# An adaptive-sum task, transfers through DRAM and the last mixed rows of a two-layer hybrid backbone on one Trainium2 core

## The chip, the cores and the metric

The kernel runs on one core of one Trainium2 chip. A core has a matrix engine (TensorE, PE in the profile; its weight loads are shown apart as PEld), VectorE (DVE), ScalarE (ACT), GpSimd (POOL) and SyncE (SP), which issues most of the transfers between DRAM and on-chip memory. Each engine carries out its own list of instructions in the order in which the program wrote them, and waits where an instruction needs something that another engine or a transfer has not finished. The measure is the device time of one execution in microseconds (us), lower being better; the time before is the median of three.

## The reference, cut to what matters

Two layers run over 256 latent tokens x and 256 context tokens ctx, each 2,048 wide, all in 32-bit floating point. Each layer starts with a normalization whose shift, scale and final gate are computed from one conditioning vector c ("adaptive" values): a product of a vector with a 2,048 x 6,144 matrix for each layer.

```python
def adaln(cond, w, b):
    m = jax.nn.silu(cond) @ w + b
    return jnp.split(m, 3, axis=-1)            # shift, scale, gate

for i in range(DEPTH):                          # DEPTH = 2
    shift, scale, gate = adaln(c, ada_w[i], ada_b[i])
    h = modulate(rms_norm(x, norm_g[i]), shift[:, None], scale[:, None])
    ...
    y = na_ssd_mixer(...) if i % 2 == 0 else short_conv_mixer(...)
    x = x + gate[:, None] * y
```

Layer 0 projects h into queries, keys, values, gates and the inputs of a state-space scan (SSD) with one large matrix; 16 heads do two-dimensional neighbourhood attention over latent and context tokens, and 32 heads of 64 do the scan in both directions. The results, 4,096 wide, are gated and the scan's half is normalized in 8 groups of 256 columns:

```python
def gated_group_rmsnorm(y, z, g):
    yz = (y * jax.nn.silu(z)).reshape(b, seq, SSD_GROUPS, -1)
    yz = yz * lax.rsqrt(jnp.mean(yz * yz, axis=-1, keepdims=True) + EPS)
    return yz.reshape(b, seq, SSD_WIDTH) * g
...
out = jnp.concatenate([ya, yb], axis=-1) @ w_out      # 4096 -> 2048
```

Layer 1 is a gated short convolution: four projections of h, a product of two of them convolved over three tokens, two gates, and an output projection.

## The kernel before

**Weights.** Each 32-bit product is made of three products of numbers split into a high and a low part. A weight tile of 512 KB is loaded by SP into one of five tiles called raw; ScalarE casts it into the high part wH (L423), VectorE subtracts that from the original into the low part wL (L430, in `low_part`), and TensorE multiplies (all products stand at L198, in the helper `mm`; transposes at L202, in `turn`). There are three buffers of wH and of wL. When `low_part` has been emitted, the raw tile is given back and `issue` emits the next load on SP. 452 such loads follow each other: layer 0's projections, then from load 228 on the output projection in three passes, and layer 1 from load 292 on, whose output projection is the last 32.

**What sets the order.** The program is written by generators ("tasks") that yield a condition before each piece: an engine, the tiles that the piece reads, and a number of PSUM banks, as in `yield W_("ACT", mx)`; "AQ" means ScalarE's DMA queue. They stand in three queues, urgent, side and back. The class `Plan` keeps a modelled clock for each engine and, for keys of 128 elements of a tile, when they were last written and read; `Plan.add` (L94 and following) advances it for each instruction emitted: a fixed cost by shape, or for a transfer a latency and the bytes at a rate. `may` decides from this model whether a task's next piece may be emitted already: the tiles must be ready, by the model, no later than about the engine's own time, which itself may run only some way ahead of TensorE (4500 ns for urgent, 2500 for side, 1500 for back). Where nothing may be emitted and the program cannot go on, `force` takes the piece that comes first. The model only fixes the order; on the chip each engine waits for what it needs. `cap` and `grow` set how many of ten tiles tmp (128x512) and nine tiles half (128x256) a task may hold.

**Adaptive sums.** The task `gemv_gen` in the queue back makes 16 vectors of 512 adaptive values, n = 0 to 15 (layer 0's gate, then layer 1's shift, scale and gate). For each it zeroes the tile acc on VectorE (L810), lets SP load a row of 512 bias values into acc's first partition (L811), and then consumes eight loads of ada_w, 512 KB each, which share the five raw tiles with the weights: two multiply-adds on VectorE per load (L820), 16 per vector. Four matmuls with ones add up the partitions, VectorE copies the result to rowb (L829) and ScalarE's queue sends it to the DRAM buffer mrow. Layer 1's start needs n = 11, its end n = 15.

**Scan groups.** For each of the 8 groups of scan heads, SP reads rows of cumulative sums from the DRAM buffer csr into tiles tmp, spread over 128 partitions (L1373, 256 KB each). ScalarE (L1383, L1390, L1393) and VectorE (L1387, L1398, L1401) make decay factors from them, and TensorE multiplies these with the inputs xtm. The group norm then takes the root on POOL (L1437), scales a 128x128 identity by it on VectorE (L1441, into a tile half), and multiplies ones with that on TensorE, so that the factor of each token stands in all partitions.

**Mixed rows.** Heads and scan groups give 32 blocks of 128 rows by 256 tokens ("mixed rows", 0 to 15 from attention and 16 to 31 from the scan), the input of the output projection. `put_mix` sends each to the DRAM buffer mixd on ScalarE's queue. Later three tasks `mixes` read them back in pairs, one tmp tile reserved to each task, and split each into high (ScalarE, L1538) and low (VectorE, L1539) in the memory where parts of h (tiles hH and hL) stood; a pair must therefore wait until these are free, which `free_rows` counts.

## Time and profile before

| what | us |
|---|---|
| median of three runs (lowest to highest) | 1801.51 (1799.98 to 1804.06) |
| time of the profiled execution | 1802.22 |
| span of the profiled execution | 1800.3 |
| TensorE busy | 1760.2 |
| VectorE busy | 1283.5 |
| ScalarE busy | 785.7 |
| POOL busy | 31.1 |
| mean granted TensorE clock | 0.998 of full |
| read from and written to DRAM | 372.89 MB and 11.96 MB |

All profile figures are of one execution. The span runs from its first to its last recorded instruction. A group of instructions is written as line, engine, operation, output<-input with buffer numbers left out, shape and type, then the number of them, their busy time in us and the mean in ns of one, and behind the second bar the idle time of the engine just before them with what ended it. A row of the timeline gives the start in us, the length, the engine, the line and the instruction; what stands in brackets is the engine's idle time before it and what ended it. In rows of waits the three numbers are the sum in us, how often, and the longest. A row of stretches gives the interval, then for PE, its weight loads, VectorE, ScalarE and POOL the busy time with the number of instructions, the idle time of all engines together, the granted TensorE clock, the DMA share and the GB/s. "SPq" is SP's DMA queue, "ACTq" ScalarE's.

### The profile page before, as it was taken

What the parts mean: (1) busy time and instruction counts of PE and PEld (TensorE: products, weight loads), DVE (VectorE), ACT (ScalarE), POOL (GpSimd) and SP (SyncE); (2) the same over time, 40 slices, a digit from 0 to 9 for tenths busy, and PEclk for the clock granted to TensorE, in tenths of its full rate; (3) what the DMA queues carried; (4) which work ended last, traced back from release to release, by engine and by line L of the source; (5) the groups of instructions that cost most, each with busy time, mean ns of one, the idle gap of its engine ahead of it and who ended that gap; (6) DMA issues with size and microseconds to landing.
All of it is one profiled execution on the core that took longest, in us unless ns stands there. A gap on an engine that the chain in (4) does not pass through costs nothing.

```text
span 1800.3 us, 25545 instructions
## 1 busy us (share of the span) xinstructions
PE 1760.2 (98%) x9545; PEld 1469.2 (82%) x9545; DVE 1283.5 (71%) x2049; ACT 785.7 (44%) x1354; POOL 31.1 (2%) x28
## 2 busy tenths in 40 slices
...
GB/s 347 340 291 254 194 168 126 156 206 194 211 161 190 162 174 204 191 158 167 172 219 120 163 188 194 232 209 295 273 184 232 260 278 268 270 237 265 220 220 167
DMA packets 260220, 385.23 MB, mean 214 GB/s; under 512 B 33424, under 2 KB 113008, under 8 KB 260096
## 3 DMA queue, kind: packets, MB, share of 16 engines
...
q14 instruction: 49, 0.40, 0.1%
HBM read 372.89 MB, written 11.96 MB: 214 GB/s over the span
## 4 chain that ended last, share of the span: by engine, by line
PE 89%; DMA 4%; DVE 4%; issue 1%; ACT 1%; SPq 0%; POOL 0%; ACTq 0%; POOLq 0%; DVEq 0%
PE bank L198 86%; PE bank L202 3%; DMA raw<-in_ada_w 2%; DVE wL L430 2%; DMA tmp<-dram_csr 1%; DVE acc L820 0%; DMA raw<-in_w_in 0%; DMA Dg<-dram_trd 0%; ACT wH L423 0%; DMA tmp<-in_x 0%; DMA xs<-in_x 0%; DVE hL L769 0%; DVE tmp L1398 0%; DVE tmp L1217 0%; DMA Du<-dram_trd 0%
## 5 line engine op out<-in xcount | busy, mean ns | idle before, releaser
L423 ACT CAST wH<-raw 128x1024 fp32r<-128x1024 f32 (+1 forms) x440 | 459.5, 1045 | 707.4 <-PE bank L198 606.5
L430 DVE TENSOR_TENSOR wL<-raw,wH 128x1024 fp32r<-128x1024 f32 (+1 forms) x440 | 530.5, 1212 | 225.9 <-ACT wH L423 224.1
L198 PE MATMUL bank<-hH,wH 128*128 128x256 f32 (+1 forms) x1040 | 342.7, 330 | 0.9 <-ACT wH L423 0.9
L198 PE MATMUL bank<-hL,wH 128*128 128x256 f32 (+1 forms) x1040 | 336.8, 324 | 0.0
L198 PE MATMUL bank<-hH,wL 128*128 128x256 f32 (+1 forms) x1024 | 331.3, 324 | 1.5 <-DVE wL L430 1.5
L198 PE MATMUL bank<-wH,h 128*128 128x512 f32 x1024 | 318.7, 392 | 2.1 <-DVE h L1662 1.7
L198 PE MATMUL bank<-wH,hH 128*128 128x512 f32 x640 | 257.2, 402 | 4.8 <-ACT hH L763 2.6
L820 DVE SCALAR_TENSOR_TENSOR acc<-raw,csil,acc 128x512 f32<-128x512 f32 x256 | 191.7, 749 | 91.0 <-DMA raw<-in_ada_w 74.0
L198 PE MATMUL bank<-wL,hH 128*128 128x512 f32 x640 | 249.8, 391 | 0.3 <-DVE wL L430 0.3
L198 PE MATMUL bank<-wH,hL 128*128 128x512 f32 x640 | 249.5, 390 | 0.1
L198 PEld LDWEIGHTS bank<-wH,h 128*128 128x128 f32 x1024 | 193.0, 189 | 44.3 <-DVE h L1662 3.0
L198 PEld LDWEIGHTS bank<-hH,wH 128*128 128x128 f32 x1040 | 197.6, 190 | 18.7 <-issue 2.0
L198 PEld LDWEIGHTS bank<-hL,wH 128*128 128x128 f32 x1040 | 197.7, 190 | 15.6
L198 PEld LDWEIGHTS bank<-hH,wL 128*128 128x128 f32 x1024 | 194.5, 190 | 17.8 <-DVE wL L430 2.5
L198 PE MATMUL bank<-wL,h 128*128 128x512 f32 x512 | 200.7, 392 | 5.4 <-DVE wL L430 5.4
L198 PE MATMUL bank<-wH,mix 128*128 128x512 f32 x512 | 162.7, 393 | 0.0
L198 PEld LDWEIGHTS bank<-wH,hH 128*128 128x128 f32 x640 | 120.2, 188 | 35.3 <-issue 6.5
L198 PEld LDWEIGHTS bank<-wH,hL 128*128 128x128 f32 x640 | 120.1, 188 | 25.6 <-DVE hL L769 0.6
L198 PEld LDWEIGHTS bank<-wL,hH 128*128 128x128 f32 x640 | 120.2, 188 | 24.8 <-DVE wL L430 1.1
L198 PEld LDWEIGHTS bank<-wL,h 128*128 128x128 f32 x512 | 96.6, 189 | 27.1 <-DVE wL L430 6.9
L198 PEld LDWEIGHTS bank<-wH,mix 128*128 128x128 f32 x512 | 96.1, 188 | 20.8 <-issue 0.9
L198 PE MATMUL bank<-wL,mix 128*128 128x512 f32 x256 | 99.8, 390 | 0.0
...
## 6 DMA issues: line engine op xcount, KB each, us to landing
...
raw<-in_sc_in SPq DMA_DIRECT2D x128, 512.0 KB, 4.4
...
tmp<-dram_csr SPq DMA_DIRECT2D x32, 256.0 KB, 6.2
...
```

The source lines that it names most:

```text
L198: E(T.matmul(o, l, r, start=start, stop=stop, skip_group_check=True))
L202: E(T.transpose(o, i, ident if k == 128 else ident[:k, :k]))
L423: E(S.copy(H, v))
L430: E(V.tensor_tensor(out=Lo, in0=v, in1=H.bitcast(F32), op=ALU.subtract))
L820: E(V.scalar_tensor_tensor(out=acc, in0=v[:, j], scalar=csil[:, 2 * k + j:2 * k + j + 1], in1=acc, op0=ALU.mult, op1=ALU.add))
```

## The change

**Plan.** In the model a transfer no longer waits for earlier writes of the tile that it writes, every transfer from or to a DRAM buffer counts as finished 3000 ns later, and the time at which a tile is written by a transfer only moves up. An engine's name with a "+" behind it ("DVE+", "ACT+") asks `may` to count the tiles as ready 1000 ns later than modelled.

**Sums.** The zeroing of acc is gone: the first of the 16 steps is a plain multiplication (tensor_scalar). The bias row goes into a tile of its own, adab, as four pieces of 128 on partitions 0, 32, 64 and 96, which POOL zeroes once at the start; it is added where the result is taken from PSUM, so the copy L829 becomes an addition of two operands. Pieces that consume a load ask for "DVE+".

**Mixed rows.** If the memory that a row goes to is already free when the row is finished, the new `place` splits it there at once, on ScalarE and VectorE, without the way through DRAM. In the order written, this is so for rows 12 to 15 and 28 to 31; the other 24 go through mixd as before and are read in 12 pairs. The tasks that read pairs take a tmp tile when they need it (`grow`, `cap`) instead of holding one each, and ask for "ACT+".

**Group norm.** The scaled identities (L1441) and the products of ones with them are replaced by transposes (`turn`) of the root's columns, each spread over 128 elements by reading with stride 0; TensorE's condition is now the root r2 itself.

Together VectorE has 16 memsets and 16 scalings fewer, and 16 of 256 multiply-adds are multiplications; ScalarE's queue has 12 reads of mixd instead of 16 and 24 writes instead of 32. TensorE's number of instructions is the same.

```diff
         for k in ko:
-            s = max(s, 0.0 if e == "PE" else self.w[k] + 60, self.r[k] + 60)
+            s = max(s, 0.0 if e == "PE" or op == "DMACopy" else self.w[k] + 60, self.r[k] + 60)
         if op == "DMACopy":
...
                 done = free = max(self.dma, s + 1000) + n / self.RATE + 1500
+            if any(a.tensor.name.startswith("dram") for a in ins + outs):
+                done = free = done + 3000
         else:
...
         for k in ko:
-            self.w[k] = done
+            self.w[k] = max(self.w[k], done) if op == "DMACopy" else done
             self.last[k[0]] = max(self.last[k[0]], done)
...
             return False
+        late = eng[-1] == "+"
+        eng = eng.rstrip("+")
         now, t = plan.t["PE"], plan.t["ACT" if eng == "AQ" else eng]
-        rdy = plan.ready(aps)
+        rdy = plan.ready(aps) + (1000 if late else 0)
         if eng == "AQ":
...
                             continue
-                        when_ = max(plan.t["ACT" if eng == "AQ" else eng], plan.ready(f))
+                        when_ = max(plan.t["ACT" if eng == "AQ" else eng.rstrip("+")], plan.ready(f))
                     if best is None or when_ < best[0]:
...
             c0 = 4096 + n * 512 if n < 4 else (n - 4) * 512
-            yield W_("DVE", nb=0)
-            E(V.memset(acc, 0.0))
-            E(DMA.dma_start(acc[:1, :], ada_b[lay:lay + 1, c0:c0 + 512]))
+            yield W_("SP")
+            E(DMA.dma_start(adab[0:128:32, :], ada_b[lay, c0:c0 + 512].rearrange("(g c) -> g c", g=4)))
             for k in range(8):
                 yield when(lambda: not (("gem", n, k) not in RAW))
-                yield W_("DVE", RAW["gem", n, k][1], acc)
+                yield W_("DVE+", RAW["gem", n, k][1])
                 raw, v = RAW.pop(("gem", n, k))
...
                         yield W_("DVE", acc)
+                    if not k + j:
+                        E(V.tensor_scalar(out=acc, in0=v[:, j], scalar1=csil[:, 0:1], scalar2=None, op0=ALU.mult))
+                        continue
                     E(V.scalar_tensor_tensor(out=acc, in0=v[:, j], scalar=csil[:, 2 * k + j:2 * k + j + 1], in1=acc,
...
             yield W_("DVE", ps)
-            E(V.tensor_copy(rowb, ps[:, :128]))
+            E(V.tensor_tensor(out=rowb, in0=ps[:, :128], in1=adab, op=ALU.add))
             give(free_b, ps)
...
     rowb = mrb = st([128, 128], "rowb")
+    adab = st([128, 128], "adab")
+    E(G.memset(adab, 0.0))
...
+    mH = [None] * 32
+
+    def place(i, o):
+        hl = st([128, 2, 256], f"hH{i}" if i < 16 else f"hL{i - 16}", F32R, name=f"mix{i}")
+        E(S.copy(hl[:, 0], o))
+        E(V.tensor_tensor(out=hl[:, 1], in0=o, in1=hl[:, 0].bitcast(F32), op=ALU.subtract))
+        mH[i] = hl
+
     def put_mix(i, o):
+        if free_rows[0] > i % 16:
+            yield W_("ACT", o)
+            place(i, o)
+            give(free_h, o)
+            return
         yield W_("AQ", o)
...
         E(G.tensor_tensor(out=r2, in0=r2, in1=mhalf[:, :2], op=ALU.pow))
-        yield W_("DVE", r2)
-        dg = half()
-        for t in range(2):
-            E(V.tensor_scalar(out=dg[:, t * 128:(t + 1) * 128], in0=ident, scalar1=r2[:, t:t + 1], scalar2=None, op0=ALU.mult))
-        yield W_("PE", dg, nb=1)
+        yield W_("PE", r2, nb=1)
         Rb = bank()
         for t in range(2):
-            mm(Rb[:, t * 128:(t + 1) * 128], ONES, dg[:, t * 128:(t + 1) * 128], t == 0, True)
-        give(free_h, dg)
+            turn(Rb[:, t * 128:(t + 1) * 128], r2[:, t:t + 1].to_broadcast([128, 128]))
         yield W_("DVE", Rb)
...
-    mH = [None] * 32
-
     def mix_gen(ip):
-        yield when(lambda: 2 * ip in written and 2 * ip + 1 in written and free_rows[0] > (2 * ip + 1) % 16)
-        yield W_("AQ", mixd[2 * ip:2 * ip + 2])
+        two_ = (2 * ip, 2 * ip + 1)
+        yield when(lambda: all(i in written or mH[i] is not None for i in two_) and free_rows[0] > (2 * ip + 1) % 16)
+        mine = [i for i in two_ if mH[i] is None]
+        if not mine:
+            return
+        yield ("grow", 1, 0)
+        yield W_("AQ", *[mixd[i] for i in mine])
         mx = tmp()
         m3 = two(mx)
-        E(DMA2.dma_start(m3, mixd[2 * ip:2 * ip + 2].rearrange("b p c -> p b c")))
-        yield W_("ACT", mx)
-        for j in range(2):
-            i = 2 * ip + j
-            hl = st([128, 2, 256], f"hH{i}" if i < 16 else f"hL{i - 16}", F32R, name=f"mix{i}")
-            E(S.copy(hl[:, 0], m3[:, j]))
-            E(V.tensor_tensor(out=hl[:, 1], in0=m3[:, j], in1=hl[:, 0].bitcast(F32), op=ALU.subtract))
-            mH[i] = hl
+        if len(mine) == 2:
+            E(DMA2.dma_start(m3, mixd[2 * ip:2 * ip + 2].rearrange("b p c -> p b c")))
+        else:
+            E(DMA2.dma_start(m3[:, mine[0] % 2], mixd[mine[0]]))
+        for i in mine:
+            yield W_("ACT+", mx)
+            place(i, m3[:, i % 2])
         give(free_t, mx)
+        yield ("cap", 0, 0)
...
     for k in range(3):
-        spawn(urgent, mixes(k), 1)
+        spawn(urgent, mixes(k))
     do_gv(3, 4)
```

The order changes in many places; lines after the change have other numbers (L430 is L434, L820 and L1383 become L826 and L1404, L1538 and L1539 now stand in `place`, L948 and L949). Three places follow. Names are those of the kernel; a number behind a name is the buffer, and "x2" means two in a row.

The first is VectorE's list at the third block of layer 1's convolution (Du, the product of two projections, comes back from DRAM there; 1577 to 1594 us in the trace before). Before:

```order
L1766 TENSOR_TENSOR tmp_108<-bank_124,tmp_112 128x4x4x32
L430 TENSOR_TENSOR wL_139<-raw_131,wH_136 128x1024
L829 COPY rowb<-bank_127 128x128
L810 MEMSET acc 128x512
L430 TENSOR_TENSOR wL_140<-raw_132,wH_137 128x1024
L820 SCALAR_TENSOR_TENSOR acc<-raw_134,csil,acc 128x512 x2
L430 TENSOR_TENSOR wL_141<-raw_133,wH_138 128x1024
L820 SCALAR_TENSOR_TENSOR acc<-raw_133,csil,acc 128x512 x2
L430 TENSOR_TENSOR wL_139<-raw_135,wH_136 128x1024
L430 TENSOR_TENSOR wL_140<-raw_131,wH_137 128x1024
```

And with the change:

```order
L1785 TENSOR_TENSOR tmp_110<-bank_124,tmp_113 128x4x4x32
L434 TENSOR_TENSOR wL_141<-raw_135,wH_138 128x1024
L434 TENSOR_TENSOR wL_139<-raw_132,wH_136 128x1024
L434 TENSOR_TENSOR wL_140<-raw_131,wH_137 128x1024
L434 TENSOR_TENSOR wL_141<-raw_133,wH_138 128x1024
L434 TENSOR_TENSOR wL_139<-raw_134,wH_136 128x1024
L434 TENSOR_TENSOR wL_140<-raw_135,wH_137 128x1024
```

The end of one sum and the begin of the next stood between the splits; now there are splits alone, since the sums come earlier in the order: the last load of n = 11 is consumed at split 222 instead of 278, that of n = 15 at 364 instead of 398.

The second is VectorE's list at the last groups of the scan (about 1130 to 1149 us in the trace before). Before:

```order
L1387 SCALAR_TENSOR_TENSOR tmp_107<-tmp_107,csl 128x128 x2
L820 SCALAR_TENSOR_TENSOR acc<-raw_134,csil,acc 128x512 x2
L1539 TENSOR_TENSOR mix_9183<-tmp_110,mix_9183 128x256
L1539 TENSOR_TENSOR mix_9186<-tmp_110,mix_9186 128x256
L1539 TENSOR_TENSOR mix_9190<-tmp_104,mix_9190 128x256
L1539 TENSOR_TENSOR mix_9193<-tmp_104,mix_9193 128x256
L1398 SCALAR_TENSOR_TENSOR tmp_107<-tmp_111,dtl,tmp_107 128x128 x2
L1401 TENSOR_TENSOR tmp_107<-tmp_107 128x256
L430 TENSOR_TENSOR wL_141<-raw_132,wH_138 128x1024
L1387 SCALAR_TENSOR_TENSOR tmp_106<-tmp_106,csl 128x128 x2
L820 SCALAR_TENSOR_TENSOR acc<-raw_134,csil,acc 128x512
L430 TENSOR_TENSOR wL_139<-raw_135,wH_136 128x1024
```

And with the change:

```order
L1419 SCALAR_TENSOR_TENSOR tmp_106<-tmp_113,dtl,tmp_106 128x128 x2
L1422 TENSOR_TENSOR tmp_106<-tmp_106 128x256
L434 TENSOR_TENSOR wL_141<-raw_135,wH_138 128x1024
L949 TENSOR_TENSOR mix_9262<-tmp_105,mix_9262 128x256
L949 TENSOR_TENSOR mix_9265<-tmp_105,mix_9265 128x256
L434 TENSOR_TENSOR wL_139<-raw_132,wH_136 128x1024
L1408 SCALAR_TENSOR_TENSOR tmp_112<-tmp_112,csl 128x128 x2
L949 TENSOR_TENSOR mix_9290<-tmp_104,mix_9290 128x256
L949 TENSOR_TENSOR mix_9293<-tmp_104,mix_9293 128x256
L949 TENSOR_TENSOR mix_9315<-tmp_105,mix_9315 128x256
L949 TENSOR_TENSOR mix_9318<-tmp_105,mix_9318 128x256
L434 TENSOR_TENSOR wL_140<-raw_133,wH_137 128x1024
```

The multiply-adds of the sums are gone from this place, and the splits of mixed pairs (mix) stand between weights; the pairs use two tmp tiles in turn.

The third is ScalarE's list at a scan group of the second block of heads (about 655 to 675 us in the trace before). Before:

```order
L423 CAST wH_136<-raw_134 128x1024
L1383 ACTIVATE tmp_104<-tmp_104,ncs 128x128 x2
L1390 ACTIVATE tmp_104<-tmp_104 128x256
L1393 ACTIVATE tmp_104<-tmp_112,dtl 128x128 x2
L1383 ACTIVATE tmp_106<-tmp_106,ncs 128x128 x2
L1390 ACTIVATE tmp_106<-tmp_106 128x256
L1393 ACTIVATE tmp_106<-tmp_112,dtl 128x128 x2
L423 CAST wH_137<-raw_135 128x1024
L1383 ACTIVATE tmp_109<-tmp_109,ncs 128x128 x2
```

And with the change:

```order
L427 CAST wH_136<-raw_134 128x1024
L1404 ACTIVATE tmp_108<-tmp_108,ncs 128x128 x2
L1411 ACTIVATE tmp_108<-tmp_108 128x256
L1414 ACTIVATE tmp_108<-tmp_112,dtl 128x128 x2
L838 DMA dram_mrow<-rowb 4x128
L427 CAST wH_137<-raw_132 128x1024
L1404 ACTIVATE tmp_105<-tmp_105,ncs 128x128 x2
L1411 ACTIVATE tmp_105<-tmp_105 128x256
L1414 ACTIVATE tmp_105<-tmp_112,dtl 128x128 x2
L1404 ACTIVATE tmp_106<-tmp_106,ncs 128x128 x2
L427 CAST wH_138<-raw_135 128x1024
```

The second and third head of the group now stand behind one more weight cast (wH), so their use of the rows from csr comes later against the weights.

## The prediction

> **What bounds the kernel now.** I read the page first, then who TensorE waited for, then the timeline around each of its idle moments, and backwards from there.
>
> ```profile
> PE 1760.2 (98%) x9545; PEld 1469.2 (82%) x9545; DVE 1283.5 (71%) x2049; ACT 785.7 (44%) x1354; POOL 31.1 (2%) x28
> ```
> ```profile
> PE bank L198 <- DMA raw<-in_ada_w: 12.9, 2, 12.7
> PE bank L198 <- DVE wL L430: 7.2, 7, 4.4
> ```
>
> TensorE is busy for 1760.2 of 1800.3 us. The change leaves the number of matmuls as it is, so only the other 40 us can move, and what idleness hides behind them. 12.9 us of it is the first load, which the change does not touch. The rest is many small waits; those that a late sum or a late DRAM read stands behind are these, in the PE timeline (start, length, instruction, idle before it):
>
> ```profile
> 210.69 0.39 PE L198 MATMUL bank<-hH,wL 128*128 128x256 f32 x1 [0.70 <-DVE wL L430]
> ...
> 669.58 0.33 PE L198 MATMUL bank<-tmp,xtm 128*64 128x128 f32 x2 [1.02 <-DVE tmp L1401]
> ...
> 675.01 0.38 PE L198 MATMUL bank<-const,half 128*128 128x1 f32 x2 [0.47 <-DVE half L1424]
> ...
> 856.66 0.39 PE L198 MATMUL bank<-hH,wL 128*128 128x256 f32 x1 [0.52 <-DVE wL L430]
> ...
> 1147.04 0.43 PE L198 MATMUL bank<-tmp,xtm 128*64 128x128 f32 x2 [1.38 <-ACT Vt L989]
> ...
> 1148.73 0.33 PE L198 MATMUL bank<-tmp,xtm 128*64 128x128 f32 x2 [1.26 <-DVE tmp L1401]
> ...
> 1555.48 0.50 PE L198 MATMUL bank<-wL,h 128*128 128x512 f32 x1 [0.81 <-DVE wL L430]
> ...
> 1586.80 0.39 PE L198 MATMUL bank<-wL,h 128*128 128x512 f32 x1
> 1587.03 0.62 PE L198 MATMUL bank<-wH,h 128*128 128x512 f32 x2
> 1587.48 0.39 PE L198 MATMUL bank<-wL,h 128*128 128x512 f32 x1
> ...
> 1593.39 0.80 PE L198 MATMUL bank<-wL,h 128*128 128x512 f32 x1 [4.38 <-DVE wL L430]
> ```
>
> A busy TensorE starts a matmul every 0.23 us and shows it for 0.39 us, so each idle figure understates the loss by 0.16 us. The largest is 4.38 us at 1593. Behind it on VectorE, in the same stretch:
>
> ```profile
> 1577.20 0.48 DVE L810 MEMSET acc<- 128x512 f32 x1
> ...
> 1582.98 1.54 DVE L820 SCALAR_TENSOR_TENSOR acc<-raw,csil,acc 128x512 f32<-128x512 f32 x2 [2.70 <-DMA acc<-in_ada_b]
> 1584.44 1.22 DVE L430 TENSOR_TENSOR wL<-raw,wH 128x1024 fp32r<-128x1024 f32 x1
> 1590.66 1.54 DVE L820 SCALAR_TENSOR_TENSOR acc<-raw,csil,acc 128x512 f32<-128x512 f32 x2 [5.00 <-DMA raw<-in_ada_w]
> 1592.11 2.35 DVE L430 TENSOR_TENSOR wL<-raw,wH 128x1024 fp32r<-128x1024 f32 x2
> ```
> ```profile
> 1585.68 0.37 SPq L393 DMA_DIRECT2D raw<-in_ada_w  x1
> ```
>
> The sum first waits 2.70 us for the bias row. That delays the split at 1584.44, whose buffer the next sum's load needs: it is issued at 1585.68 and lands 5 us later, and VectorE, which works in order, holds two more weight splits behind it. The idleness then costs a second time, in the granted clock (column after the engines, in stretches):
>
> ```profile
> 1593.40:1598.20 4.80, 4.80 (x11) 3.79 (x12) 3.42 (x4) 0.00 (x0) 0.00 (x0) 0.50 0.98 342
> 1598.20:1603.00 4.80, 4.80 (x22) 3.92 (x21) 3.38 (x6) 3.71 (x6) 0.00 (x0) 0.99 0.40 133
> ```
>
> 11 matmuls against 22 in equal time: 2.4 us more.
>
> **The change part by part.** *Bias at eviction and margin.* One row of each price involved, from the groups by line and shape, and SP's wait for the memset (total, times, longest):
>
> ```profile
> L820 DVE SCALAR_TENSOR_TENSOR acc<-raw,csil,acc 128x512 f32<-128x512 f32 x256 | 191.7, 749 | 91.0 <-DMA raw<-in_ada_w 74.0 <-issue 8.2 <-DMA acc<-in_ada_b 5.0
> ...
> L1046 DVE TENSOR_SCALAR tmp<-tmp,s 128x512 f32<-128x512 f32 x32 | 15.6, 487 | 1.1
> ...
> L810 DVE MEMSET acc<- 128x512 f32 x16 | 7.8, 485 | 0.9
> ...
> L829 DVE COPY rowb<-bank 128x128 f32<-128x128 f32 x16 | 4.6, 286 | 10.4 <-PE bank L198 10.4
> ...
> L1441 DVE TENSOR_SCALAR half<-const,r 128x128 f32<-128x128 f32 x16 | 3.9, 283 | 4.3 <-POOL r L1437 4.3
> ...
> L198 PE MATMUL bank<-half,const 128*128 128x128 f32 x36 | 5.8, 279 | 0.1
> ...
> L202 PE MATMUL bank<-const,half 128*128 128x128 f32 x32 | 6.2, 276 | 1.0 <-ACT half L733 1.0
> ```
> ```profile
> SPq L811 <- DVE acc L810: 15.7, 13, 4.1
> ```
>
> VectorE loses 16 memsets (7.8 us), 16 diagonal scalings (3.9 us) and 16 x (0.749 - 0.487) = 4.2 us on first products: 15.9 us of 1283.5. The added row costs between nothing over the copy's 286 ns and one more such copy, 16 x 0.29 = 4.6 us; I take 1 us, since the shape stays. None of it counts by itself: VectorE has 29% free. What counts is that nothing in a sum waits for the row's round trip any more, and that SP's queue, with the weight loads behind it, no longer stands 15.7 us for memsets; the new row load waits only for the previous sum's last addition, which is several splits earlier in the order. The 16 matmuls against a diagonal (279 ns as the profile shows one) become 16 transposes of the same tile (276 ns): bounds of twice and half that time are +4.5 and -2.2 us, and I take 0 by the second row. What they read is now one column broadcast, which no row here shows. PE waits for POOL's root directly, one VectorE step earlier than before. The zeroing of the new bias tile stands on POOL at the start, beside the 12.9 us of the first load: 0, and even without that cover no more than the 0.5 us of a memset four times as wide.
>
> The margin itself asks the plan to believe a sum's load 1 us later. Its price is that a load holds its raw tile for longer; the number of such tiles that sums may hold at a time (one or two of five) is unchanged, so a weight load can be late by no more than it could before. It gives between nothing (if the loads come later by as much) and L820's whole 74.0 us on VectorE, of which only what reaches PE counts.
>
> By the order, VectorE reaches 19 of the last 32 sum loads in before with five undivided weight loads ahead of them on SP, and none in the change; 23 stand at four instead. One weight is 12 matmuls, 12 x 0.227 = 2.7 us. L820's 50 waits average 74.0 / 50 = 1.5 us. So I take the middle of that: the waits of 1 to 2 us go, those of 4 to 5 us keep half. And the order has no sum left near the third Du block, where the 4.38 us arose, since the last sum ends 34 weights earlier. That place, and the 0.81 us before it, I take whole: 4.38 + 0.81 + 2 x 0.16 + 2.4 = 7.9 us.
>
> Two more hang on sums, by these rows: at 210 a sum waited for its own load, at 850 for the row (its releaser reads "issue").
>
> ```profile
> 207.97 1.54 DVE L820 SCALAR_TENSOR_TENSOR acc<-raw,csil,acc 128x512 f32<-128x512 f32 x2 [4.09 <-DMA raw<-in_ada_w]
> ...
> 849.93 1.54 DVE L820 SCALAR_TENSOR_TENSOR acc<-raw,csil,acc 128x512 f32<-128x512 f32 x2 [3.14 <-issue]
> ```
>
> In the change the sum at the same place uses a load that is one older, and the row is gone: 0.70 + 0.52 + 0.32 = 1.5 us, taken whole.
>
> *Time for DRAM, and rows placed directly.* The plan had given a 256 KB read on SP about 3 us (1 us, 262144 bytes at its 270 per ns, 1 us). The trace, timeline and issues (last column: us to landing):
>
> ```profile
> 656.98 0.97 SPq L1373 DMA_DIRECT2D tmp<-dram_csr  x2
> ...
> 663.09 0.70 ACT L1383 ACTIVATE tmp<-tmp,ncs 128x128 f32<-128x128 f32 x2 [1.97 <-DMA tmp<-dram_csr]
> ```
> ```profile
> tmp<-dram_csr SPq DMA_DIRECT2D x32, 256.0 KB, 6.2
> ...
> tmp<-dram_mixd ACTq DMA_DIRECT2D x16, 256.0 KB, 4.7
> ```
>
> 6.2 us is 3 us more, just what is added. These late rows end in the idleness at 669 and 675; at 1147 the bank that PE needs is freed by ScalarE, which had stood for a mixed pair, and at 1149 VectorE had stood for sums. The order puts PE's use of the decay blocks of 669 and 1149 some 20 matmuls (20 x 0.227 = 4.5 us) later against the weights, and no sum among the last groups. Together 1.02 + 0.47 + 1.38 + 1.26 + 4 x 0.16 = 4.8 us. Between nothing and all of it I take three quarters, 3.6 us, as each of these chains has other links. The Trainium skill speaks against this part: its page "DMA: Bandwidth & Descriptors", Latency and other measured facts, puts a DMA's fixed cost at about 2 us, which was the plan's old figure; by it the added 3 us are too many, readers stand late for nothing, and the 3.6 us would be 0 and the time 1794.1 us. The 6.2 us row disagrees with it.
>
> Placing eight rows directly takes eight 128 KB writes and four pair reads from the queues; casts and subtractions stay 32 each. The cast now waits on ScalarE for the row's own product, with weight casts behind it, but the order sets these rows at least three splits ahead of their use, 8 us: 0. If that cover failed, each would cost PE a cast and a subtraction, 0.4 us apiece by half of the 0.70 and 0.76 us shown below for two.
>
> *What comes new.* Everything in layer 1 is reordered, so waits of this kind will appear elsewhere. Bounds: none, or as much again as the six small ones above (6.3 us). I take two of 1 us. The layer boundary keeps its own chain, a step of which is
>
> ```profile
> 1351.33 0.50 PE L198 MATMUL bank<-wH,h 128*128 128x512 f32 x1 [1.42 <-DVE h L1662]
> ```
>
> The order of VectorE there is the same, without the row and the memset at its head; I count 0.
>
> **Sum.** The profiled execution took 1802.2 us, 0.7 above the median. 7.9 + 1.5 + 3.6 - 2.0 = 11.0 us off: 1791.2, in median terms 1790.5 us. All gained and nothing new: 1787.3, and with the boundary's 1.4 + 0.16 and some of its neighbours, 1785. Half of it: 1796.
>
> **Rivals.** *The DRAM time does nothing*: consumers move later in the order and their products with them, so PE's waits at 669, 675, 1147 and 1149 stay; the 3.6 us are not gained, 1794.1 us. For it: each of these chains passes three engines in turn after the read. Against: the 1.97 us that ScalarE stood for the read itself, and a landing of 6.2 us that only the new figure matches. (The Trainium skill's fixed cost, in the page and section above, would make it so; the row of 6.2 us bears it out little.)
>
> *VectorE becomes the bound.* The sums finish 34 weights earlier, so layer 1 takes them up: between weights 180 and 200 the order has 12 loads instead of 5, 7 x 2 x 0.749 = 10.5 us. Fully on the path, with a half-clock spell, 12.9 us: 1802.2 - 13.0 + 12.9 - 0.7 = 1801.4, no change. Against it, its busy time in that stretch (the third engine's figure):
>
> ```profile
> 950.00:1000.00 50.00, 50.00 (x293) 43.52 (x290) 31.74 (x54) 24.93 (x64) 4.07 (x2) 1.00 0.48 139
> ```
>
> 18 us of 50 are free.
>
> *Mixed pairs hold up the first output pass: slower.* Their tasks no longer reserve a tile each; in the order the first eight reads use two tiles in turn, so a read waits on ScalarE's queue until the pair two before is divided, and the weight casts stand behind it.
>
> ```profile
> 1131.91 0.70 ACT L1538 CAST mix<-tmp 128x256 fp32r<-128x256 f32 x2
> ...
> 1132.33 0.76 DVE L1539 TENSOR_TENSOR mix<-tmp,mix 128x256 fp32r<-128x256 f32 x2 [4.24 <-ACT mix L1538]
> ```
>
> One round is 4.7 + 0.70 + 0.76 = 6.2 us; wholly on the path three of them (18.5 us) outweigh the full 14.2 us gain and the 0.2% (3.6 us) that a measurement can tell; four give 1790.5 + 24.6 = 1815. Against: two tiles in turn make 3.1 us a pair, a pair's two weights last 5.4 us, and the order places every pair at least two splits ahead of its use.
>
> **How the numbers follow.** Forecast 0.60, DRAM time useless 0.15, VectorE bound 0.14, mixed pairs 0.11. Faster by over 0.2% (below 1797.9): 0.74, most of the first two; same 0.15; slower 0.11. The likeliest's own range is 1785 to 1796; the range reaches to the no-change case, 1785 to 1801.
>
> **What would show it.** L820's wait for in_ada_w falls from 74 us to 20 to 40; no wait on a bias row; ScalarE's waits for csr and mixd go to near 0; PE waits on wL under 3 us; no clock of 0.50 after the start; VectorE near 1269 us busy; the boundary's 1.4 us remains. Wrong: a new PE wait over 3 us with half clock, a tile of mix among PE's releasers, or wL waits in layer 1 above 3 us.

## The result, and the profile after

The changed kernel takes 1793.17 us (median of 10 runs, 1791.27 to 1796.46) against 1803.94 us of the kernel before in 10 runs (1799.98 to 1809.95). The ratio is 0.9937 with a 95% interval of 0.9925 to 0.9950: faster by 0.63%, which is 11.4 us of 1803.94. The prediction had 11.0 us off. The profiled execution of the changed kernel took 1791.9 us with a span of 1789.3 us, 11.0 us shorter than the span before. So the total agrees almost to the figure; the experiments below show that the terms of the sum do not.

The page's busy line, and the rows of waits in the changed kernel that answer to those shown of before (total, times, longest; L200 is `mm`, L434 the split into wL, L1404 the first use of csr rows on ScalarE):

```profile
PE 1755.4 (98%) x9529; PEld 1465.3 (82%) x9529; DVE 1269.0 (71%) x2017; ACT 786.4 (44%) x1354; POOL 32.2 (2%) x29
```
```profile
PE bank L200 <- DVE wL L434: 4.5, 7, 1.5
PE bank L200 <- DMA raw<-in_ada_w: 13.0, 2, 12.8
ACT tmp L1404 <- DMA tmp<-dram_csr: 6.5, 5, 2.4
```

VectorE has lost 14.5 us of work and TensorE 4.8 us of recorded time. TensorE's longest wait on a weight split is 1.5 us where it was 4.4. The groups by line and shape:

```profile
L826 DVE SCALAR_TENSOR_TENSOR acc<-raw,csil,acc 128x512 f32<-128x512 f32 x240 | 179.8, 749 | 26.1 <-DMA raw<-in_ada_w 22.1
L824 DVE TENSOR_SCALAR acc<-raw,csil 128x512 f32<-128x512 f32 x16 | 7.7, 480 | 2.9 <-DMA raw<-in_ada_w 2.9
L835 DVE TENSOR_TENSOR rowb<-bank,adab 128x128 f32<-128x128 f32 x16 | 4.6, 289 | 20.5 <-PE bank L200 20.5
L204 PE MATMUL bank<-const,r 128*128 128x128 f32 x16 | 3.0, 271 | 0.0
...
L200 PE MATMUL bank<-half,const 128*128 128x128 f32 x4 | 0.9, 299 | 0.1
```

VectorE stands 25.0 us (22.1 + 2.9) for loads of sums instead of 74.0, and nothing waits for a bias row. The eviction with a second operand takes 289 ns where the copy took 286. The group norm's products are 16 records of 3.0 us; before, they stood among the 36 of the row of 5.8 us, of which 4 (0.9 us) are left: 32 records, two for each multiplication with a scaled identity, against one for a transpose, and 1.9 us less. That is why TensorE shows 16 records fewer (9529 against 9545), though the program has as many products as before.

The third block of layer 1's convolution, where 4.38 us were idle, now in stretches (interval; PE, its weight loads, VectorE, ScalarE, POOL; then granted clock, DMA share, GB/s):

```profile
1575.00:1585.00 10.00, 10.00 (x46) 8.28 (x45) 4.68 (x4) 4.00 (x4) 0.00 (x0) 1.00 0.92 238
1585.00:1595.00 10.00, 10.00 (x46) 8.26 (x45) 8.54 (x15) 5.82 (x8) 0.00 (x0) 1.00 0.50 155
```

TensorE is busy throughout at full clock. Measured by the weight casts on ScalarE, which both kernels do in the same number: before the 361st cast the change is 2.6 us ahead of the kernel before, at the 381st 10.2 us. So 7.6 us of the 11.0 come from this one place; from the 350th cast on (2.0 us ahead), which takes in the 0.81 us shortly before it, they are 8.2. Over the weights before it there is a balance of gains and new losses. The new idle moments of TensorE in layer 0, from its timeline:

```profile
246.33 0.39 PE L200 MATMUL bank<-hH,wL 128*128 128x256 f32 x1 [0.55 <-DVE wL L434]
```
```profile
375.15 0.66 PE L204 MATMUL bank<-const,tmp 128*128 128x128 f32 x4 [1.01 <-DVE tmp L1363]
```
```profile
429.95 0.38 PE L200 MATMUL bank<-hH,wL 128*128 128x256 f32 x1 [1.05 <-DVE wL L434]
```
```profile
698.62 0.39 PE L200 MATMUL bank<-hH,wL 128*128 128x256 f32 x1 [1.48 <-DVE wL L434]
```
```profile
1180.71 0.50 PE L200 MATMUL bank<-wL,mix 128*128 128x512 f32 x1 [0.67 <-DVE wL L434]
```

With 0.16 us each for the overlap of records they make 5.6 us; those of before at 210, 669, 675, 856, 1147 and 1149 (6.3 us in the same count) are gone.

### The profile page after: what moved, and what is told of

Read it like the earlier page. It is cut to its first block, busy times and chain, and to the rows that moved or that the text cites. A ratio compares the mean times of both kernels' runs of the same rounds, so it can differ in the third digit from the quotient of the medians.

```text
span 1789.3 us, 25450 instructions
## 1 busy us (share of the span) xinstructions
PE 1755.4 (98%) x9529; PEld 1465.3 (82%) x9529; DVE 1269.0 (71%) x2017; ACT 786.4 (44%) x1354; POOL 32.2 (2%) x29
## 4 chain that ended last, share of the span: by engine, by line
PE 92%; DVE 3%; DMA 2%; ACT 1%; issue 1%; SPq 0%; POOL 0%; POOLq 0%; DVEq 0%; ACTq 0%
PE bank L200 89%; PE bank L204 3%; DVE wL L434 1%; DMA raw<-in_ada_w 1%; DMA raw<-in_w_out 1%; ACT wH L427 0%; DMA half<-in_rows 0%; DMA tmp<-dram_exr 0%; DMA xs<-in_x 0%; DVE hL L773 0%; DVE h L1681 0%; DVE tmp L769 0%; ACT h L1700 0%; ACT hH L767 0%; DVE xm L633 0%
## 5 line engine op out<-in xcount | busy, mean ns | idle before, releaser
L434 DVE TENSOR_TENSOR wL<-raw,wH 128x1024 fp32r<-128x1024 f32 (+1 forms) x440 | 532.3, 1214 | 275.9 <-ACT wH L427 274.4
L200 PE MATMUL bank<-hH,wH 128*128 128x256 f32 (+1 forms) x1040 | 342.7, 330 | 0.9 <-ACT wH L427 0.9
L200 PE MATMUL bank<-hL,wH 128*128 128x256 f32 (+1 forms) x1040 | 336.9, 324 | 0.0
L200 PE MATMUL bank<-hH,wL 128*128 128x256 f32 (+1 forms) x1024 | 331.6, 324 | 3.4 <-DVE wL L434 3.3
L200 PE MATMUL bank<-wH,h 128*128 128x512 f32 x1024 | 317.0, 390 | 2.1 <-DVE h L1681 1.7
L200 PE MATMUL bank<-wH,hH 128*128 128x512 f32 x640 | 257.8, 403 | 4.8 <-ACT hH L767 2.6
L200 PE MATMUL bank<-wL,hH 128*128 128x512 f32 x640 | 249.8, 391 | 0.3 <-DVE wL L434 0.3
L200 PE MATMUL bank<-wH,hL 128*128 128x512 f32 x640 | 249.4, 390 | 0.1
L200 PEld LDWEIGHTS bank<-wH,h 128*128 128x128 f32 x1024 | 191.9, 188 | 43.8 <-DVE h L1681 2.9
L200 PEld LDWEIGHTS bank<-hH,wH 128*128 128x128 f32 x1040 | 197.8, 190 | 18.0 <-issue 1.6
L200 PEld LDWEIGHTS bank<-hH,wL 128*128 128x128 f32 x1024 | 194.6, 190 | 20.2 <-DVE wL L434 4.6
L200 PEld LDWEIGHTS bank<-hL,wH 128*128 128x128 f32 x1040 | 197.9, 190 | 15.1
L200 PE MATMUL bank<-wL,h 128*128 128x512 f32 x512 | 199.4, 389 | 0.2 <-DVE wL L434 0.2
L826 DVE SCALAR_TENSOR_TENSOR acc<-raw,csil,acc 128x512 f32<-128x512 f32 x240 | 179.8, 749 | 26.1 <-DMA raw<-in_ada_w 22.1
L200 PE MATMUL bank<-wH,mix 128*128 128x512 f32 x512 | 162.6, 393 | 0.0
L200 PEld LDWEIGHTS bank<-wH,hH 128*128 128x128 f32 x640 | 120.1, 188 | 36.1 <-issue 7.2
L200 PEld LDWEIGHTS bank<-wH,hL 128*128 128x128 f32 x640 | 120.1, 188 | 25.6 <-DVE hL L773 0.6
L200 PEld LDWEIGHTS bank<-wL,hH 128*128 128x128 f32 x640 | 120.2, 188 | 24.5 <-DVE wL L434 1.1
L200 PEld LDWEIGHTS bank<-wL,h 128*128 128x128 f32 x512 | 96.1, 188 | 20.5 <-DVE wL L434 0.6
L200 PEld LDWEIGHTS bank<-wH,mix 128*128 128x128 f32 x512 | 96.1, 188 | 20.2 <-issue 0.4
L200 PE MATMUL bank<-wL,mix 128*128 128x512 f32 x256 | 99.9, 390 | 0.7 <-DVE wL L434 0.7
```

Of the source, the lines that this page charges most:

```text
L200: E(T.matmul(o, l, r, start=start, stop=stop, skip_group_check=True))
L434: E(V.tensor_tensor(out=Lo, in0=v, in1=H.bitcast(F32), op=ALU.subtract))
L826: E(V.scalar_tensor_tensor(out=acc, in0=v[:, j], scalar=csil[:, 2 * k + j:2 * k + j + 1], in1=acc, op0=ALU.mult, op1=ALU.add))
```

## The experiments

Each was timed against the kernel before on the same chip; ratios are to the kernel before, with their 95% intervals.

| kernel | ratio | interval | TensorE's longest wait after the first 100 us, us |
|---|---|---|---|
| changed kernel | 0.9937 | 0.9925 to 0.9950 | 1.48 |
| order as before, bias at eviction | 1.0002 | 0.9989 to 1.0014 | 4.19 |
| order as before, sums read zeros | 0.9935 | 0.9922 to 0.9949 | 1.39 |
| before, plan's rate 268 | 0.9986 | 0.9977 to 0.9995 | 6.53 |
| before, new sums alone | 0.9968 | 0.9959 to 0.9977 | 3.89 |
| before, new DRAM time alone | 1.0031 | 1.0019 to 1.0042 | 4.89 |
| before, new mixed rows alone | 1.0082 | 1.0062 to 1.0102 | 6.43 |
| changed, old mixed rows | 0.9993 | 0.9984 to 1.0003 | 9.14 |
| changed, no margin | 0.9991 | 0.9981 to 1.0000 | 1.63 |
| changed, old DRAM time | 0.9938 | 0.9925 to 0.9950 | 1.77 |
| changed, old group norm | 0.9945 | 0.9932 to 0.9958 | 1.39 |
| changed, plan's rate 268 | 0.9919 | 0.9907 to 0.9932 | 1.39 |
| changed, margin 2000 ns | 0.9899 | 0.9886 to 0.9913 | 1.42 |

The waits are of one profiled execution each. The 1.4 us at the layer boundary stand in every one but that with new mixed rows alone, which has 2.17 us there.

### The bias row's round trip, in an unchanged order

```diff
-            E(DMA.dma_start(acc[:1, :], ada_b[lay:lay + 1, c0:c0 + 512]))
+            ab = adab[n % 2]
+            DMA.dma_start(ab[0:128:32, :], ada_b[lay, c0:c0 + 512].rearrange("(g c) -> g c", g=4))
+            plan.as_row(acc[:1, :])        # the plan's clocks move as for the row before
...
-            E(V.tensor_copy(rowb, ps[:, :128]))
+            E(V.tensor_tensor(out=rowb, in0=ps[:, :128], in1=ab, op=ALU.add))
```

> The kernel before with its order of instructions kept word for word on every engine; only the bias row goes to a tile of its own (two tiles in turn) and is added at eviction, so that no sum waits for the row's round trip (the zeroing of acc stays). If the row's wait is a cause of the idle 4.38 us at 1593: VectorE's 2.70 us at 1583 go, the split whose raw tile the next sum's load needs comes 2.7 us earlier, TensorE's wait there falls from 4.38 to about 1.7 us and the half-clock spell (2.4 us) goes with it: 5 us, with the 0.7 us of the wait at 856 some 5.5 us less than before, ratio 0.997. If only the order counts (sums too near to their loads): the 4.38 us stay within 0.5 us and the ratio is 0.999 to 1.000.

Measured: 1.0002. The row's wait is gone from VectorE, and the wait of TensorE is still there. VectorE's timeline, SP's queue and TensorE's timeline at the place (L833 is the multiply-add, L441 the split, L404 the loads):

```profile
1578.03 0.48 DVE L821 MEMSET acc<- 128x512 f32 x1
...
1581.32 1.53 DVE L833 SCALAR_TENSOR_TENSOR acc<-raw,csil,acc 128x512 f32<-128x512 f32 x2
1582.77 1.22 DVE L441 TENSOR_TENSOR wL<-raw,wH 128x1024 fp32r<-128x1024 f32 x1
1591.29 1.54 DVE L833 SCALAR_TENSOR_TENSOR acc<-raw,csil,acc 128x512 f32<-128x512 f32 x2 [7.31 <-DMA raw<-in_ada_w]
```
```profile
1584.01 0.37 SPq L404 DMA_DIRECT2D raw<-in_ada_w  x1
```
```profile
1594.02 0.50 PE L209 MATMUL bank<-wL,h 128*128 128x512 f32 x1 [4.19 <-DVE wL L441]
```

Counted from the memset in each trace (1578.03, and 1577.20 before), the split and the issue of the load come 2.5 us earlier than in the kernel before (the load 6.0 us behind the memset instead of 8.5). But VectorE goes on only 0.2 us earlier (13.3 instead of 13.5 us behind the memset): it stood 7.31 us instead of 5.00. In stretches of the same execution:

```profile
1584.00:1588.00 4.00, 4.00 (x19) 3.33 (x18) 0.00 (x0) 2.10 (x2) 0.00 (x0) 1.00 1.06 289
1588.00:1590.00 2.00, 1.83 (x9) 1.18 (x7) 0.00 (x0) 0.36 (x1) 0.00 (x0) 1.00 1.04 293
1590.00:1593.00 3.00, 0.00 (x0) 0.00 (x0) 1.67 (x3) 0.69 (x1) 0.00 (x0) 1.00 0.05 14
```

The DMA engines are fully busy until 1590 and then idle, since the loads that come next need raw tiles that VectorE has not given back. By these rows the load waited for the transfers that were on their way, not for its issue. The step of the prediction that began the 4.38 us with the 2.70 us for the row falls. So does the other one that hung on a row: the 0.52 us at 856 stay (857.19 here), although the sum before them no longer waits (847.35 instead of 849.93). VectorE then stands 3.37 us for ScalarE instead and is no earlier at the split.

### No waiting for loads of sums, in an unchanged order

```diff
-                    E(V.scalar_tensor_tensor(out=acc, in0=v[:, j], scalar=csil[:, 2 * k + j:2 * k + j + 1], in1=acc,
-                                             op0=ALU.mult, op1=ALU.add))
+                    sc = csil[:, 2 * k + j:2 * k + j + 1]
+                    V.scalar_tensor_tensor(out=acc, in0=zero, scalar=sc, in1=acc, op0=ALU.mult, op1=ALU.add)
+                    plan.as_sum([v[:, j], sc, acc], acc)     # the plan's clocks move as before
```

> The kernel before with its order kept word for word on every engine; the sums' multiply-adds read a tile of zeros instead of the loaded part of ada_w (so the adaptive values are wrong, which changes no time), and the loads are issued as before. VectorE then never waits for a load of a sum. If this waiting is what starves TensorE in layer 1: the 4.38 us at 1593 with their half-clock spell go, the 0.7 us at 210 too: 8 to 9 us less, ratio 0.995 to 0.996. If the transfers themselves are behind there (they are busy for 0.85 to 1.0 of the time up to the wait): the weight comes late all the same, 2 us or more of the wait stay, ratio 0.998 to 1.000.

Measured: 0.9935, or 1794.02 us, as much off as the whole change. The group of multiply-adds and TensorE's waits on a split:

```profile
L839 DVE SCALAR_TENSOR_TENSOR acc<-zero,csil,acc 128x512 f32<-128x512 f32 x256 | 191.5, 748 | 14.1 <-DMA acc<-in_ada_b 10.2
```
```profile
PE bank L216 <- DVE wL L448: 1.3, 4, 0.5
```

The work on VectorE is the same (191.5 us) and the loads are still made; the waiting for them is gone, and with it the idleness at 1593. The edit takes away a second thing: SP no longer waits for the multiply-adds before it fills a raw tile again (174.2 us in 117 waits before). At 1593 that was not what TensorE lacked, for in the kernel before ScalarE had cast two more weights by 1589.9, and only their splits on VectorE were missing until 1592.11:

```profile
1586.10 1.05 ACT L423 CAST wH<-raw 128x1024 fp32r<-128x1024 f32 x1 [0.87 <-PE bank L198]
1588.82 1.04 ACT L423 CAST wH<-raw 128x1024 fp32r<-128x1024 f32 x1 [1.67 <-PE bank L198]
```

So VectorE, standing in order for a sum's load, is what starved TensorE there. The ratio is lower than either theory had it (11.7 us off, against 8 to 9); the spans of the two profiled executions differ by 6.6 us, and where the rest of the 11.7 goes stands in no trace. The waits at 670 (1.2 us), 857 (0.5 us) and 1148 (0.9 us) stay, so they did not hang on sums' loads; the 1.38 us at 1147 fall to 0.57.

### A meaningless new order of the kernel before

```diff
-    RATE = 270.0
+    RATE = 268.0
```

> The kernel before with one number of the plan changed by less than one per cent (transfer rate 268 instead of 270 bytes per ns), which means nothing but orders some instructions otherwise: a sample of what a new order alone does. If the wait at 1593 belongs to the sums' chain: some wait of 3 us or more behind a sum's load stays in layer 1, ratio 0.998 to 1.002. If it was an accident of one order: gone, ratio 0.995 to 0.997.

Measured: 0.9986. The wait at 1593 is gone in this order, which has no part of the change, and another has come in the first pass of the output projection, where ScalarE stood for a mixed pair:

```profile
1241.12 0.79 PE L198 MATMUL bank<-wH,mix 128*128 128x512 f32 x1 [6.53 <-ACT mix L1538]
```

Neither expectation held: not a sum's wait that stays, nor a gain that remains. Where the large wait falls changes with the order; one order alone can't show whether there is always one.

### The new sums alone

```diff
-            yield W_("DVE", nb=0)
-            E(V.memset(acc, 0.0))
-            E(DMA.dma_start(acc[:1, :], ada_b[lay:lay + 1, c0:c0 + 512]))
+            yield W_("SP")
+            E(DMA.dma_start(adab[0:128:32, :], ada_b[lay, c0:c0 + 512].rearrange("(g c) -> g c", g=4)))
...
+                    if not k + j:
+                        E(V.tensor_scalar(out=acc, in0=v[:, j], scalar1=csil[:, 0:1], scalar2=None, op0=ALU.mult))
+                        continue
...
-            E(V.tensor_copy(rowb, ps[:, :128]))
+            E(V.tensor_tensor(out=rowb, in0=ps[:, :128], in1=adab, op=ALU.add))
```

> The kernel before with the new sums alone (no zeroing, bias at eviction) and no margin, no new DRAM time, no direct rows, old group norm; the plan orders anew and the last sum ends at split 331. If the sums' own chain is what the 8 us in layer 1 hung on: TensorE's waits at 1555 and 1593 and the half clock are gone, 8 us less, ratio 0.9955. If the margin is what does it: a wait on wL of over 2 us behind a sum stays somewhere in layer 1, and the ratio is 0.998 to 1.000.

Measured: 0.9968, half of the gain. Layer 1 runs without a wait over 0.2 us behind its boundary, as the first theory has it. What it gains there is partly lost at the last scan groups:

```profile
1149.68 1.19 PE L198 MATMUL bank<-tmp,xtm 128*64 128x128 f32 x8 [3.89 <-ACT Vt L993]
```

There ScalarE and VectorE wait for each other among scan groups and mixed pairs (VectorE stood 2.31 us for a pair's cast just before).

### The new DRAM time alone

```diff
-            s = max(s, 0.0 if e == "PE" else self.w[k] + 60, self.r[k] + 60)
+            s = max(s, 0.0 if e == "PE" or op == "DMACopy" else self.w[k] + 60, self.r[k] + 60)
...
+            if any(a.tensor.name.startswith("dram") for a in ins + outs):
+                done = free = done + 3000
...
-            self.w[k] = done
+            self.w[k] = max(self.w[k], done) if op == "DMACopy" else done
```

> The kernel before with the new time for DRAM transfers in the plan alone (3000 ns, no waiting for earlier writes). By the prediction's sum: the four waits behind late rows (669, 675, 1147, 1149) go, 3.6 us, and new ones of about 2 us come; the 4.38 us at 1593 stay, since the sums are as before: ratio 0.998 to 0.9995. If any new order of layer 1 loses the wait at 1593 (it was an accident of one order): 6 to 10 us less, ratio 0.9945 to 0.9965.

Measured: 1.0031, slower, outside both expectations. The waits at 669, 675, 1147 and 1149 are gone, as the first said, and the one at 1593, as the second said, but three others came (3.70, 2.64 and 4.89 us), two of them here:

```profile
433.98 0.39 PE L200 MATMUL bank<-hH,wL 128*128 128x256 f32 x1 [3.70 <-DVE wL L432]
```
```profile
1245.82 0.79 PE L200 MATMUL bank<-wH,mix 128*128 128x512 f32 x1 [4.89 <-ACT mix L1540]
```

The first is a sum again: VectorE stood 2.85 us for its load at 431. The second is a mixed pair. The one not shown, 2.64 us at 708, has VectorE standing twice (2.06 and 1.30 us) for rows from a DRAM buffer.

### The new mixed rows alone

```diff
     def put_mix(i, o):
+        if free_rows[0] > i % 16:
+            yield W_("ACT", o)
+            place(i, o)
+            give(free_h, o)
+            return
...
+        yield ("grow", 1, 0)
...
-        yield W_("ACT", mx)
+            yield W_("ACT+", mx)
...
-        spawn(urgent, mixes(k), 1)
+        spawn(urgent, mixes(k))
```

> The kernel before with the new treatment of mixed rows alone (eight rows placed directly, tasks that take a tmp tile when needed, margin for the split of pairs). Seen so far: three orders that differ from the one before all lost the 4.38 us at 1593, and each got a wait of 3.9 to 6.5 us on the way of the mixed rows instead. If that exchange is the point, these rows are the cure: the wait at 1593 goes (8 us), no wait over 2 us comes between 1140 and 1250: ratio 0.994 to 0.996. If the rows are hidden anyway, as the prediction counted (0 us), and each order simply has one large wait somewhere: ratio 0.997 to 1.001 with a wait of 3 us or more in another place.

Measured: 1.0082, much slower, and so both theories missed. Three waits, the last two behind loads of sums (VectorE stood 5.72 and 6.10 us for them); the third is the one of 1593, at the same place in the order:

```profile
1163.32 0.80 PE L198 MATMUL bank<-wL,mix 128*128 128x512 f32 x1 [4.01 <-DVE wL L432]
```
```profile
1430.61 0.80 PE L198 MATMUL bank<-wL,h 128*128 128x512 f32 x1 [6.43 <-DVE wL L432]
```
```profile
1609.91 0.79 PE L198 MATMUL bank<-wL,h 128*128 128x512 f32 x1 [4.05 <-DVE wL L432]
```

The first is what the prediction's slower rival described: VectorE stood for a pair's cast with two weight splits queued behind it.

```profile
1161.37 0.76 DVE L943 TENSOR_TENSOR mix<-tmp,mix 128x256 fp32r<-128x256 f32 x2 [3.08 <-ACT mix L942]
1162.05 2.35 DVE L432 TENSOR_TENSOR wL<-raw,wH 128x1024 fp32r<-128x1024 f32 x2
```

### The changed kernel with the old mixed rows

```diff
     def put_mix(i, o):
-        if free_rows[0] > i % 16:
-            yield W_("ACT", o)
-            place(i, o)
-            give(free_h, o)
-            return
...
-        yield ("grow", 1, 0)
...
-        yield ("cap", 0, 0)
...
-        spawn(urgent, mixes(k))
+        spawn(urgent, mixes(k), 1)
```

> The changed kernel with all 32 mixed rows through DRAM again and a tmp tile reserved to each of the three tasks; the rest of the change stays, the margin too. If the mixed rows are what the other parts lack: a wait of 3.5 us or more on a late pair between 1140 and 1250 with a spell of lower clock, 4 to 8 us more than the changed kernel, ratio to the kernel before 0.996 to 0.998. If they are hidden: 0.993 to 0.9945.

Measured: 0.9993. Nearly the whole gain is lost, more than expected, and one wait shows where; ScalarE's queue, ScalarE and TensorE:

```profile
1228.09 0.93 ACTq L954 DMA_DIRECT2D dram_mixd<-half  x2
...
1235.98 0.44 ACTq L1547 DMA_DIRECT2D tmp<-dram_mixd  x1
1242.10 0.71 ACT L948 CAST mix<-tmp 128x256 fp32r<-128x256 f32 x2 [7.55 <-DMA tmp<-dram_mixd]
```
```profile
1242.56 0.79 PE L200 MATMUL bank<-wH,mix 128*128 128x512 f32 x1 [9.14 <-ACT mix L948]
```

The last two rows are written to DRAM at 1228; the pair is read at 1236, the next transfer on ScalarE's queue, and its cast begins 6.1 us later. TensorE's last matmul before the wait began at 1233.03, so it stood idle before the read was even issued. Most of the two trips falls into a stretch in which the DMA engines are busy all the time (shares 1.06 and 1.04):

```profile
1232.00:1236.00 4.00, 1.42 (x7) 0.84 (x5) 1.09 (x1) 1.04 (x1) 0.00 (x0) 0.92 1.06 402
1236.00:1240.00 4.00, 0.00 (x0) 0.00 (x0) 0.00 (x0) 0.00 (x0) 0.00 (x0) 0.50 1.04 389
```

The rows finished last are those that make the trip with nothing to hide it, and rows finished late are what the changed kernel places directly. The run also gives each task its tmp tile back; that this matters too is not excluded, but the wait shown is for the trip.

### The changed kernel without margin

```diff
-        rdy = plan.ready(aps) + (1000 if late else 0)
+        rdy = plan.ready(aps) + (0 if late else 0)
```

> The changed kernel with the margin of 1000 ns set to nothing, for sums and pairs; the rest stays. By the prediction VectorE's waits for loads of sums rise again from 22 to about 50 us or more, and some 3 us of them reach TensorE as waits on wL: ratio to the kernel before 0.995 to 0.9965. If the margin only moves the waits about: 0.993 to 0.9945, though VectorE waits as long.

Measured: 0.9991, more lost than expected (median 1802.55 us of 12 runs, 1798.17 to 1806.66). VectorE's waits for sums' loads are back:

```profile
DVE acc L826 <- DMA raw<-in_ada_w: 69.3, 40, 5.1
PE bank L200 <- DVE wL L434: 6.6, 11, 1.6
```

The profiled execution was the fastest of the 12, 4.4 us below the median. Even it has a span 7.1 us longer than the changed kernel's, without one wait over 1.7 us after the first 100 us: from there to the layer boundary TensorE has nine idle moments of 0.4 us or more, 8.4 us together, where the changed kernel has five with 4.8 us. Where the typical run loses its further microseconds stands in no trace; a lower clock does not explain them, for three of the runs at a mean granted clock of 1.000 took 1802.8 to 1803.7 us. That VectorE, with 69 us of waits of up to 5.1 us, lets more through when loads land a little later is only an argument. The margin's value, 0.54%, is measured, in one order; its two uses, for sums and for pairs, were not tried apart.

### The changed kernel with the old DRAM time

```diff
-            s = max(s, 0.0 if e == "PE" or op == "DMACopy" else self.w[k] + 60, self.r[k] + 60)
+            s = max(s, 0.0 if e == "PE" else self.w[k] + 60, self.r[k] + 60)
...
-            if any(a.tensor.name.startswith("dram") for a in ins + outs):
-                done = free = done + 3000
...
-            self.w[k] = max(self.w[k], done) if op == "DMACopy" else done
+            self.w[k] = done
```

> The changed kernel with the plan's old times for transfers through DRAM (no 3000 ns, waiting for earlier writes); sums, margin, direct rows and group norm as changed. By the prediction's term: ScalarE's waits for csr rise from 6.5 to some 19 us and TensorE loses 3.6 us: ratio to the kernel before 0.9955. If the DRAM time does nothing: 0.993 to 0.9945. If, as in the single parts, one missing part lets a large wait in: a wait of 3.5 us or more, ratio 0.9965 to 1.000.

Measured: 0.9938, the changed kernel's ratio to 0.0001. ScalarE waits more for these rows, as expected:

```profile
ACT tmp L1402 <- DMA tmp<-dram_csr: 18.0, 12, 4.2
```

Some of it reaches TensorE. VectorE, held up by the read for which ScalarE stood until 942.54, works without a pause from 942.98 to the product (L1443) that TensorE waits for:

```profile
942.54 0.70 ACT L1402 ACTIVATE tmp<-tmp,ncs 128x128 f32<-128x128 f32 x2 [3.49 <-DMA tmp<-dram_csr]
```
```profile
948.91 0.60 PE L198 MATMUL bank<-const,half 128*128 128x1 f32 x4 [1.77 <-DVE half L1443]
```

So a late row does cost TensorE time in this order, but the changed kernel's waits on weight splits (0.55 to 1.48 us) are mostly absent from it: idle moments of 0.4 us or more between 100 us and the layer boundary come to 5.6 us here and 4.8 us there. The new time moves the waits more than it removes them. At the places of the four old waits (669, 675, 1147 and 1149) none of 0.4 us comes back with the old time.

### The changed kernel with the old group norm

```diff
-        yield W_("PE", r2, nb=1)
+        yield W_("DVE", r2)
+        dg = half()
+        for t in range(2):
+            E(V.tensor_scalar(out=dg[:, t * 128:(t + 1) * 128], in0=ident, scalar1=r2[:, t:t + 1], scalar2=None, op0=ALU.mult))
+        yield W_("PE", dg, nb=1)
...
-            turn(Rb[:, t * 128:(t + 1) * 128], r2[:, t:t + 1].to_broadcast([128, 128]))
+            mm(Rb[:, t * 128:(t + 1) * 128], ONES, dg[:, t * 128:(t + 1) * 128], t == 0, True)
```

> The changed kernel with the old group norm (scaled identities on VectorE, ones multiplied with them). The prediction gave this edit 0 us: 0.9937. The trace after shows 16 transposes at a spacing of 0.11 us where 32 records of the same spacing stood, 1.7 us on TensorE: 0.9945 to 0.995. If a new order again lets a large wait in (3 us or more): 0.996 to 0.999.

Measured: 0.9945 (0.9932 to 0.9958). This is about what 1.7 us would give, but the interval holds the changed kernel's 0.9937 too: it can't be told from nothing.

### Two more orders of the changed kernel

```diff
-    RATE = 270.0
+    RATE = 268.0
```

> The changed kernel with the plan's rate at 268 instead of 270 bytes per ns: another order with the same parts. If the parts make the plan robust: no wait of TensorE over 2.5 us after the start, ratio to the kernel before 0.992 to 0.995. If the changed kernel merely has a lucky order: a wait over 3 us comes, ratio 0.996 to 0.999.

```diff
-        rdy = plan.ready(aps) + (1000 if late else 0)
+        rdy = plan.ready(aps) + (2000 if late else 0)
```

> The changed kernel with a margin of 2000 instead of 1000 ns for sums and pairs. If the margin works by keeping VectorE and ScalarE from standing for late transfers: VectorE's waits for loads of sums fall from 22 to under 12 us and no wait of TensorE over 1.5 us comes after the start, ratio to the kernel before 0.991 to 0.9940. If more margin only moves the sums later into layer 1, where they collide again: a wait of 3 us or more there, ratio 0.996 to 0.999.

Measured: 0.9919 and 0.9899. So the change holds up in another order, and twice the margin beats both kernels: 1786.65 us (1785.96 to 1787.45) against 1804.55 us. In it:

```profile
DVE acc L826 <- DMA raw<-in_ada_w: 12.5, 12, 2.5
PE bank L200 <- DVE wL L434: 2.1, 4, 1.3
```

VectorE's waits for sums' loads are half of the changed kernel's 25.0 us. Between 220 us and the layer boundary one idle moment of TensorE is left, 1.34 us at 697. The waits came out at 12.5 us where under 12 was expected, and TensorE's longest at 1.42 us, under the 1.5. These waits of VectorE are not the whole measure: at rate 268 they are 36.5 us, more than in the changed kernel, and that order is faster.

## Why the prediction was right, and where not

**Total and direction** were right: 11.0 us forecast, 11.4 measured by the ratio, inside the range of the likeliest case.

**The wait at 1593 (7.9 us, taken whole)** was the right place and the right size: 8.2 us between the 350th and the 381st weight, which takes in both of its waits. Its cause, VectorE standing in order for a sum's load, is shown by the run with the order kept and the waiting taken away. The chain the prediction drew was wrong in its first link: the bias row's 2.70 us were no cause, since without them 4.2 us stayed, with the DMA engines busy until 1590. It is also not the change alone that moves it: a rate changed by under one per cent loses it as well, and so does the DRAM time alone. That no sum stands there any more the prediction had read off the new order; that the wait fell there at all was a trait of the old one.

**Bias at eviction and margin** were one term. The runs part them. The row's round trip is worth nothing by itself in the old order (1.0002). The margin is worth 0.54% in the new one. The prediction said that the margin "gives between nothing and L820's whole 74.0 us on VectorE"; it turned 69.3 us of waits at these multiply-adds into 22.1, inside the 20 to 40 that the prediction named. **The two at 210 and 850 (1.5 us)**: the 0.70 us at 210 hung on a sum's load, as it said, and went when the waiting was taken away; the 0.52 us at 856 did not hang on the row, and that they are gone in the changed kernel belongs to the new order.

**DRAM time (3.6 us)** failed as a price. The four waits that it was to remove are gone, but their places stay free of them without it too; taking the new time back costs nothing that can be measured (0.9938), and added alone it makes the kernel slower (1.0031). The first rival, that it does nothing, given 0.15, was right on the worth of the part and not on the mechanism: by it these four waits were to stay. Its own time, 1794.1, came out close only because other terms were off too. Of the signs that the prediction named, ScalarE's waits for mixd are gone (8.4 us before), and those for csr fell from 18.9 to 6.5 us, not to near 0.

**Mixed rows (0 us)** was the largest miss. The prediction asked whether a row placed directly could come too late, found three splits of cover and wrote 0; for the trip through DRAM that the row is spared it set no gain at all. Without this part the changed kernel has 9.14 us of idleness for the last pair and a ratio of 0.9993. In the order of the kernel before no such wait occurs; in the orders with the other rate and with the DRAM time alone it does, with 6.53 and 4.89 us. The prediction priced the part by the waits of one order, though the change makes another.

**The slower rival (mixed pairs hold up the first output pass, 0.11)** did not come in the changed kernel, whose largest wait on that way is 0.67 us, but its mechanism came where the rows were changed alone (4.01 us at 1163). **VectorE as the bound** did not come: its busy time is 1269.0 us as forecast, and between 950 and 1000 us, where the sums moved, TensorE has no wait of half a microsecond.

**Group norm (0 us)**: 1.9 us less on TensorE by the rows, though the run with the old norm can't tell it from nothing; the old trace had two records for each product, 32 of the 36 in the row that the prediction quoted, and the prediction read them as 16. **New waits (2.0 us)** were 5.6 us. **The boundary's 1.4 us** stayed.

Put together from the two traces: 7.9 + 1.5 + 4.8 us of old waits gone, 1.9 us of transposes, less 5.6 us of new ones: 10.5 us, against 11.0 in the spans; the remaining 0.5 us were not followed. The sum of the prediction met it by luck: its too small gains (4.8 taken at three quarters, 1.9 at nothing) and its too small new waits (3.6 us short) nearly cancelled, and mixed rows and margin, without either of which the gain is lost, stand in it at nothing and inside another term.

The parts do not add up. Alone they gave -0.32% (sums without margin), +0.31% (DRAM time) and +0.82% (mixed rows with their margin); all together, with the sums' margin and the group norm, they give -0.63%. The changed kernel with the old sums was not run. Much goes with whether an order is left with a wait of several microseconds. Of the five kernels with the old sums and their loads, four have a wait of 3.7 us or more behind a sum (4.38, 4.19, 3.70, 6.43, the first two in the same order; the one with rate 268 has none); of the eight with the new sums none has a wait over 1.7 us on a weight split. Of the five orders with the old mixed rows, four have 3.9 us or more in the stretch where these are read (3.89, 4.89, 6.53, 9.14; the order before has 1.38); of the seven with the new ones, one (4.01, the rows alone). The changed kernel has both, and the orders that keep sums, rows and a margin keep the gain (0.9938, 0.9945, 0.9919, 0.9899). But large waits are not all: without the margin, sums and rows are as new, no wait is over 1.7 us, and the gain is lost (0.9991). Margin and mixed rows were each taken out in one order only. A meaningless new order moved the ratio by 0.14% (kernel before) and 0.18% (changed kernel), a third or less of the 0.54% and 0.56% lost there; that speaks against a mere shift, but a second order would be the test.
